# Two stores issued at once from two queues in a rotation by 180 degrees

**The chip, the cores and the metric.** The kernel runs on one core of a Trainium2 chip. The metric is the device time of one execution in microseconds (us). A program on one core has no second die to compare with, so a run counts as fast when it is within 1.5% of the fastest of its kernel; a run that stands alone has an unknown state. The span of a profile is some 1.8 us shorter than the time of the same execution.

## The reference

```python
def setup_inputs():
    batch, c, h, w = 32, 3, 256, 256
    return {"x": np.random.randn(batch, c, h, w).astype(np.float32)}

def reference(x):
    return np.rot90(x, k=2, axes=(-2, -1)).astype(np.float32)
```

There are 96 images of 65536 numbers. A rotation by 180 degrees is each image read backwards.

## The kernel before

The images go in three groups of 32. A group fills a buffer of 128 partitions: image n lies in partitions 4n to 4n+3, and a partition holds one contiguous quarter of 16384 numbers (64 KB). `inside` reverses each quarter with VectorE copies through a small buffer T, and the store writes the four quarters of each image in reverse order.

```python
    # ... cut: shapes and buffers; E = 16384 numbers per partition, J = 2048;
    # back(t, lo, hi) is columns lo to hi of t backwards, copy is a VectorE copy
    def load(t, g, lo, hi, queue=nc.sync):
        return queue.dma_start(out=t[:, lo:hi], in_=x4[g][:, lo:hi])

    def store(t, g, lo, hi):
        return nc.sync.dma_start(
            out=o4[g][:, ::-1, lo:hi], in_=t[:, lo:hi])

    def inside(t):
        for lo in range(0, E // 2, J):
            hi = E - lo - J
            copy(T[:, :], back(t, hi, hi + J))
            copy(t[:, hi:hi + J], back(t, lo, lo + J))
            copy(t[:, lo:lo + J], T[:, :])

    TAIL = 1536
    HEAD = 512
    load(A, 0, 0, HEAD, nc.scalar)
    load(A, 0, HEAD, E)
    load(Bt, 1, 0, E)
    body = load(Ct, 2, 0, E - TAIL)
    load(Ct, 2, E - TAIL, E)
    inside(A)
    LEAD = 128
    store(A, 0, 0, LEAD)
    first = store(A, 0, LEAD, E)
    tc.add_manual_dep(
        first.ins, body.ins.name,
        mybir.DependencyInfo(mybir.DependencyClass.Sync, mybir.DependencyReason.DATA),
        reason="the first store is queued while the last strip is on its way")
    for g, t in ((1, Bt), (2, Ct)):
        inside(t)
        store(t, g, 0, E)
```

Four names are used below. The head is the first 512 columns of A, loaded through ACT's queue. The body is the long part of Ct's load, the strip its last 1536 columns (rows of 6 KB). The lead is the store of A's first 128 columns (rows of 512 B), which waits in SyncE's queue behind the loads.

Of the kernel before, what the change touches and what calls it, by code (L numbers as in the profile page):

```python
# [2 lines left out]

os.environ.setdefault("NEURON_RT_ULTRASERVER_MODE", "4")

# [4 lines left out]


@with_exitstack
def kernel(
    ctx: ExitStack,
    tc: tile.TileContext,
    x: bass.AP,
    out: bass.AP,
):








    nc = tc.nc
    P = 128

    B, C, H, W = x.shape
    L = H * W
    G = 32
    E = L // 4
    J = E // 8

    x4 = x.rearrange("b c h w -> (b c) (h w)").rearrange(
        "(g n) (s e) -> g (n s) e", n=G, s=4)
    o4 = out.rearrange("b c h w -> (b c) (h w)").rearrange(
        "(g n) (s e) -> g n s e", n=G, s=4)  # L40

    pool = ctx.enter_context(tc.tile_pool(name="slots", bufs=1))
    A = pool.tile([P, E], x.dtype, tag="A")
    Bt = pool.tile([P, E], x.dtype, tag="B")
    Ct = pool.tile([P, E], x.dtype, tag="C")
    T = pool.tile([P, J], x.dtype, tag="T")

    def back(t, lo, hi):
        return t[:, hi - 1:(lo - 1 if lo else None):-1]

    def copy(dst, src):
        tc.keep_in_program_order(nc.vector.tensor_copy(out=dst, in_=src))  # L52

    def load(t, g, lo, hi, queue=nc.sync):
        return queue.dma_start(out=t[:, lo:hi], in_=x4[g][:, lo:hi])  # L55

    def store(t, g, lo, hi):
        return nc.sync.dma_start(
            out=o4[g][:, ::-1, lo:hi], in_=t[:, lo:hi])

    def inside(t):
        for lo in range(0, E // 2, J):
# [12 lines that stand above are left out]
    inside(A)  # L75
    LEAD = 128
    store(A, 0, 0, LEAD)
    first = store(A, 0, LEAD, E)
    tc.add_manual_dep(
        first.ins, body.ins.name,  # L80
        mybir.DependencyInfo(mybir.DependencyClass.Sync, mybir.DependencyReason.DATA),
        reason="the first store is queued while the last strip is on its way")
    for g, t in ((1, Bt), (2, Ct)):
        inside(t)
        store(t, g, 0, E)


# [1 line left out]
_INS = ['x']  # L89
_OUTS = [((32, 3, 256, 256), 'float32')]  # L90


# [23 lines left out]
```

## Time and profile before

| | before |
|---|---|
| time, median of 3 runs (lowest to highest) | 122.11 us (121.89 to 122.15) |
| span | 120.2 us |
| packet time of q1 (SyncE) and q10 (ACT), share of 16 DMA engines | 97.0% + 0.6% |
| VectorE busy | 44.2 us, 37% |

The prediction shows the lines of this profile that carry the argument.

### The profile page before, as it was taken

The numbers are of one execution on the slowest core, as the hardware profiler recorded it, in microseconds if no ns is written. First come the engines' busy times: TensorE is split into PE (matmuls) and PEld (weight loads), VectorE is DVE, ScalarE is ACT, GpSimd is POOL, SyncE is SP. The second block draws the span as 40 slices with busy tenths as digits, with TensorE's granted clock in tenths as the row PEclk, the third lists the DMA queues.
The fourth block names the chain that finished last, engine by engine and source line by source line (L and its number), as shares of the span: only waits on it lengthen the run. The fifth ranks groups of instructions, "written<-read, shape, count | busy, mean of one in ns | idle before, by whom it ended". The sixth has DMA issues, their size and how long they took to land.

```text
span 120.2 us, 97 instructions
## 1 busy us (share of the span) xinstructions
DVE 44.2 (37%) x36; POOL 0.2 (0%) x4
## 2 busy tenths in 40 slices
DVE  0000000499995099999059999500000000000000
POOL 0000000000000000000000000000000000000000
DMA  9888988899889879979499777988898889888990
GB/s 338 349 349 349 698 349 349 360 654 393 349 349 633 382 316 553 395 316 633 178 452 693 346 346 346 693 349 349 349 698 349 349 349 698 349 349 349 654 393 0
DMA packets 1296, 50.33 MB, mean 419 GB/s; under 512 B 144, under 2 KB 272, under 8 KB 528
## 3 DMA queue, kind: packets, MB, share of 16 engines
q1 hardware_dynamic: 1152, 50.07, 97.0%
q10 hardware_dynamic: 144, 0.26, 0.6%
HBM read 25.17 MB, written 25.17 MB: 419 GB/s over the span
## 4 chain that ended last, share of the span: by engine, by line
DMA 34%; DVE 25%; another core or an unknown queue 4%; issue 1%; SPq 0%; DVEq 0%
DMA Bt<-in_x_dram 34%; DVE T L52 8%; DVE Bt L52 8%; DVE Ct L52 8%; SPq L55 0%; DVEq L52 0%
## 5 line engine op out<-in xcount | busy, mean ns | idle before, releaser
L52 DVE COPY T<-A 128x2048 f32<-128x2048 f32 x4 | 4.9, 1226 | 22.7 <-DMA A<-in_x_dram 22.6
L52 DVE COPY T<-Ct 128x2048 f32<-128x2048 f32 x4 | 4.9, 1227 | 4.5 <-DMA Ct<-in_x_dram 4.4
L52 DVE COPY T<-Bt 128x2048 f32<-128x2048 f32 x4 | 4.9, 1226 | 4.4 <-DMA Bt<-in_x_dram 4.3
L52 DVE COPY Bt<-Bt 128x2048 f32<-128x2048 f32 x4 | 4.9, 1227 | 0.1
L52 DVE COPY A<-A 128x2048 f32<-128x2048 f32 x4 | 4.9, 1227 | 0.1
L52 DVE COPY A<-T 128x2048 f32<-128x2048 f32 x4 | 4.9, 1227 | 0.1
L52 DVE COPY Bt<-T 128x2048 f32<-128x2048 f32 x4 | 4.9, 1227 | 0.1
L52 DVE COPY Ct<-T 128x2048 f32<-128x2048 f32 x4 | 4.9, 1227 | 0.1
L52 DVE COPY Ct<-Ct 128x2048 f32<-128x2048 f32 x4 | 4.9, 1227 | 0.1
L100 POOL MEMSET const-bfloat16-1.0<- 128x1 bf16 x1 | 0.1, 101 | 0.0
L100 POOL MEMSET const-uint8-127<- 128x1 uint8 x1 | 0.1, 101 | 0.0
L100 POOL MEMSET const-float32-0.0<- 128x1 f32 x1 | 0.1, 98 | 0.2 <-issue 0.2
L100 POOL MEMSET const-float32-1.0<- 128x1 f32 x1 | 0.1, 98 | 0.0
## 6 DMA issues: line engine op xcount, KB each, us to landing
out_dram<-A SPq DMA_DIRECT2D x1, 8128.0 KB, 21.1
A<-in_x_dram SPq DMA_DIRECT2D x1, 7936.0 KB, 21.9
Ct<-in_x_dram SPq DMA_DIRECT2D x1, 7424.0 KB, 57.9
Ct<-in_x_dram SPq DMA_DIRECT2D x1, 768.0 KB, 59.3
A<-in_x_dram ACTq DMA_DIRECT2D x1, 256.0 KB, 22.0
out_dram<-A SPq DMA_DIRECT2D x1, 64.0 KB, 35.2
Bt<-in_x_dram SPq DMA_DIRECT2D x1, 40.8
out_dram<-Bt SPq DMA_DIRECT2D x1, 39.8
```

The lines of the kernel that those rows point to most:

```text
L52: tc.keep_in_program_order(nc.vector.tensor_copy(out=dst, in_=src))
L100: nc = _bacc.Bacc("TRN2", target_bir_lowering=False, num_devices=1)
```

## The change

The intent is to run the first two stores side by side: A's on SyncE's queue as before, Bt's on ACT's. Both are held until the body has landed, so that neither gets among the loads. Ct's store stays on SyncE's queue.

```diff
--- before.py
+++ after.py
@@ -54,9 +54,9 @@
     def load(t, g, lo, hi, queue=nc.sync):
         return queue.dma_start(out=t[:, lo:hi], in_=x4[g][:, lo:hi])
 
-    def store(t, g, lo, hi):
-        return nc.sync.dma_start(
-            out=o4[g][:, ::-1, lo:hi], in_=t[:, lo:hi])
+    def store(t, g, lo, hi, queue=nc.sync):
+        return tc.keep_in_program_order(queue.dma_start(
+            out=o4[g][:, ::-1, lo:hi], in_=t[:, lo:hi]))
 
     def inside(t):
         for lo in range(0, E // 2, J):
@@ -75,14 +75,18 @@
     inside(A)
     LEAD = 128
     store(A, 0, 0, LEAD)
-    first = store(A, 0, LEAD, E)
-    tc.add_manual_dep(
-        first.ins, body.ins.name,
-        mybir.DependencyInfo(mybir.DependencyClass.Sync, mybir.DependencyReason.DATA),
-        reason="the first store is queued while the last strip is on its way")
-    for g, t in ((1, Bt), (2, Ct)):
-        inside(t)
-        store(t, g, 0, E)
+    inside(Bt)
+
+    def held(dma):
+        tc.add_manual_dep(
+            dma.ins, body.ins.name,
+            mybir.DependencyInfo(mybir.DependencyClass.Sync, mybir.DependencyReason.DATA),
+            reason="the stores are queued while the last strip is on its way")
+
+    held(store(A, 0, LEAD, E))
+    held(store(Bt, 1, 0, E, nc.scalar))
+    inside(Ct)
+    store(Ct, 2, 0, E)
 
 
 # ---- launch: one core; inputs and outputs as the reference has them ----
```

## The prediction

> **What bounds the kernel now.** The kernel moves three groups of images, 8.39 MB each, from HBM into the buffers A, Bt and Ct, reverses each row of 16384 numbers inside the buffer with VectorE copies, and stores the buffers with the rows of each image in reverse order. I read the page's busy row and its DMA part first, to see which resource has no room.
>
> ```profile
> DVE 44.2 (37%) x36; POOL 0.2 (0%) x4
> ...
> DMA packets 1296, 50.33 MB, mean 419 GB/s; under 512 B 144, under 2 KB 272, under 8 KB 528
> ...
> q1 hardware_dynamic: 1152, 50.07, 97.0%
> q10 hardware_dynamic: 144, 0.26, 0.6%
> ```
>
> VectorE works for 37% of the span, while the packets of the two DMA queues take 97.0 + 0.6 = 97.6% of the time of all 16 DMA engines (q1 belongs to SyncE, q10 to ACT). The packet counts say how a transfer is cut: nine DMAs of 144 packets each, which is one packet for each of the 128 partitions and 16 small ones (the 144 under 512 B) that end it on the 16 engines. So a large DMA is 8 whole rows of about 64 KB on each engine. In the trace's packet records a row of 65536 B takes 2.418 us, in either direction: 27.1 GB/s for an engine, 434 GB/s for 16.
>
> Next the order of the transfers, from the page's list of DMA issues, put together with the start of each issue in the timeline.
>
> ```profile
> out_dram<-A SPq DMA_DIRECT2D x1, 8128.0 KB, 21.1
> A<-in_x_dram SPq DMA_DIRECT2D x1, 7936.0 KB, 21.9
> Ct<-in_x_dram SPq DMA_DIRECT2D x1, 7424.0 KB, 57.9
> Ct<-in_x_dram SPq DMA_DIRECT2D x1, 768.0 KB, 59.3
> A<-in_x_dram ACTq DMA_DIRECT2D x1, 256.0 KB, 22.0
> out_dram<-A SPq DMA_DIRECT2D x1, 64.0 KB, 35.2
> Bt<-in_x_dram SPq DMA_DIRECT2D x1, 40.8
> out_dram<-Bt SPq DMA_DIRECT2D x1, 39.8
> ```
>
> ```profile
> 59.63 0.55 SPq L58 DMA_DIRECT2D out_dram<-A  x1
> 60.27 0.55 SPq L58 DMA_DIRECT2D out_dram<-Bt  x1
> 61.55 1.23 DVE L52 COPY T<-Ct 128x2048 f32<-128x2048 f32 x1 [4.40 <-DMA Ct<-in_x_dram]
> ...
> 76.68 0.54 SPq L58 DMA_DIRECT2D out_dram<-Ct  x1
> ```
>
> Issue plus landing time gives: A loaded at 22.6, Bt at 1.18 + 40.8 = 42.0, the long part of Ct at 1.63 + 57.9 = 59.5, its last strip at 2.11 + 59.3 = 61.4; A stored at 59.63 + 21.1 = 80.7, Bt at 60.27 + 39.8 = 100.1, Ct at 76.68 + 42.7 = 119.4. The landings step by 19.4 us, and 8 rows at 2.418 us are 19.34 us: six groups pass through one first-in-first-out stream without a hole. The packet records confirm it: the first data packet starts at 1.755 us, the last completion packet at 119.05 us, and the packets in between fill the 16 engines but for 0.06 us on the average engine. Thus 120.2 us = 1.76 before the first packet + 117.3 of packets + 1.13 after the last. The pure floor of bytes is 50.33 MB / 434 GB/s = 116.0 us. In the chain of waits this looks as if VectorE carried a quarter of the span; those copies lie beside transfers that fill the engines anyway.
>
> **What the Trainium skill says.** Four places bear on it. "DMA: Bandwidth & Descriptors", section "Issuing engines are not separate DMA queues", says that transfers from SyncE and ACT end up on the same 16 DMA engines and interleave, and that a second issuer only saves issue time. Its section "Where 436 GB/s comes from" puts the ceiling at 435.2 GB/s; this trace, with 434 GB/s inside a packet, sits on it. Its section "Queues, rings and completion order" says each DMA engine goes round robin between queues and switches at packet boundaries. The trace agrees and shows the grain: the 256 KB head of A, alone in ACT's queue and worth 8 x 0.084 us per engine, lands 22.0 us after its issue, with A's 7936 KB body (21.9 us), because on each engine its 2 KB rows go one at a time between the body's 62 KB rows, in bursts about 2.4 us apart (4.8, 7.2, 9.6 ... 21.7 us). Last, "Latency and other measured facts" tells of HBM copies that slow when rows of a tile lie at large power-of-two pitches; the two stores that now run together lie exactly 8.39 MB apart, but no record of this kernel shows a slowdown, and I use it only for a rival.
>
> **The change, part by part.**
>
> 1. *Bytes and rows.* Nothing removed, nothing added: nine DMAs, 50.33 MB, 36 copies of 1.227 us. Change 0 us.
>
> 2. *Bt's store goes to ACT's queue.* SyncE's second issue (0.55 us at 60.27) disappears from SyncE and about 0.5 us appears on ACT, which has been idle since 1.1 us. It was hidden: A's store had 8 x 2.40 = 19.2 us of rows in front of it. Gain 0 us.
>
> 3. *The handover from loads to stores.* The hold ends at the same event, the landing of Ct's long part. Now A's rows arrive 60.843 - 59.63 = 1.21 us after the issue starts, when the engines are just finishing the strip and the 64 KB lead; the earliest engine waits some 0.17 us, the rest less. With both issues at about 59.6, Bt's rows come at about the same 60.8. If two simultaneous issues hinder each other, this could cost an estimated 0.1 to 0.3 us; the pair of issues at 0.73 us (0.38 and 0.39 us, each as long as a lone one) speaks against it. I choose +0.1 us.
>
> 4. *The strip's landing.* This is where something moves. At 60.8 us some engines still have a strip packet in flight and its 4-byte completion unsent, and it now takes turns with 64 KB rows of Bt. Each turn costs 2.42 us. By the records, only completions or at most one strip row are unstarted at 60.8, so one or two turns: the strip lands at 61.5 + 2.4 to 4.9 = 63.9 to 66.4 rather than 61.5. Ct's twelve copies take 76.68 - 61.55 = 15.13 us, so its store is issued at 79 to 81.6 instead of 76.7.
>
> 5. *Does that delay cost?* A and Bt together keep the engines in work from 60.8 to 60.8 + 16 rows x 2.41 = 99.4, with the small remainders about 99.7. Ct's store must be issued 1.2 us before: by 98.4. The slack is 98.4 - 76.7 = 21.7 us. Even all eight strip rows of an engine, one turn each, would cost 8 x 2.42 = 19.4 us. Hidden in either case: 0 us.
>
> 6. *The end.* Ct's eight rows are last and alone, as before: 99.7 + 19.35 = 119.05, then the same 1.13 us. A and Bt share turns, so A lands near 100 rather than 80.7; nobody needs it.
>
> Sum: 122.11 + 0.1 - 0 = about 122.2; I put 122.1, since +0.1 is no larger than the spread of the three runs (121.89 to 122.15).
>
> **The rivals.**
>
> *Two queues are faster than one.* For it, only that SyncE's queue carries 97.0% of the packet time and ACT's lies idle. Against it: that time belongs to engines which both queues share, the rows leave no gap, and the end of one DMA costs one 9 ns packet. It cannot give 2%: 2.4 us is nearly all there is outside the packets (1.76 + 1.13 us), and neither piece is touched. It would make 121.9.
>
> *The strip waits so long that Ct's store comes late.* For it, the head of A, held up to 22 us by the same turns. Against it, the 21.7 us of slack. If it happened with several microseconds over, 124 to 126.
>
> *Alternating stores write slower,* through the 8.39 MB offset or through a cost at each change of queue. Against it: 16 engines already write at 16 places at once, and the alternation of the head and A's body left no measurable idle time from 5 to 21 us. A 5% loss over the 39 us in which two stores run would be 2 us: 124.
>
> *The copies of Ct are put behind the stores by the new program order.* Those stores are issued at 60, before Ct lands: nothing.
>
> **Range and chances.** Gains end at 0.2 us; plausible losses are 0.1 to 0.3 us at the handover; the rivals with 2 us or more get 3% together. So 122.1, with 121.7 to 122.5 for 8 in 10; faster by over 2% 0.5%, within 2% 96.5%, slower 3%.
>
> **What the profile afterwards would show.** Right: ACT's queue q10 with 288 packets and 8.65 MB, its share up by 128 x 2.42 / (16 x 120.2) = 16.1 points to about 16.7%, q1 down to about 81%, the sum still 97 to 98% (step 1); the issues of A and Bt both near 59.6 (step 3); the first copy of Ct at 63.9 to 66.4 and its store issued at 79 to 81.6 (step 4); A and Bt both landing some 40 us after issue (step 6); Ct's store landing at 119.4. Wrong would be: rows of stores longer than 2.42 us, holes in the DMA row near 60 or 100 us, or Ct's store issued after 98.

## More of the kernel before

The stretches view has, after the stretch and its length, the busy time of VectorE and GpSimd in it, the granted clock, the DMA share and the GB/s. A packet is counted where it starts, so a share can pass 1 when many long rows start in one stretch. This is the kernel before, from 60 us on:

```profile
60.00:80.00 20.00, 14.72 (x12) 0.00 (x0) 1.00 1.01 434
80.00:90.00 10.00, 0.00 (x0) 0.00 (x0) 1.00 1.17 505
90.00:100.00 10.00, 0.00 (x0) 0.00 (x0) 1.00 1.01 439
100.00:118.00 18.00, 0.00 (x0) 0.00 (x0) 1.00 0.94 408
```

All 16 engines are full through the whole store phase, whether VectorE works (60 to 80 us) or not.

## The result, and the profile after

| | before | after |
|---|---|---|
| median of 6 fast runs (lowest to highest) | 122.01 us (121.89 to 122.15) | 122.07 us (121.98 to 122.12) |
| ratio, 95% interval | | 1.0004 (0.9991 to 1.0017) |
| span of the profile | 120.2 us | 120.3 us |

A ratio is the mean time of one kernel's fast runs over the mean of the other's of the same rounds, so it is not quite the ratio of the medians. The change does nothing to the time that six runs can show.

The queues of the kernel after, with packets, MB and share of the 16 engines' time:

```profile
q1 hardware_dynamic: 1008, 41.68, 80.9%
q10 hardware_dynamic: 288, 8.65, 16.7%
```

Bt's store, 8.39 MB, has moved to ACT's queue, and the sum is 97.6% as before. Its list of DMA issues (KB, us from issue to landing) and its timeline at the handover from loads to stores:

```profile
out_dram<-A SPq DMA_DIRECT2D x1, 8128.0 KB, 40.5
...
out_dram<-Bt ACTq DMA_DIRECT2D x1, 40.6
```

```profile
59.78 0.55 SPq L58 DMA_DIRECT2D out_dram<-A  x1
59.81 0.61 ACTq L58 DMA_DIRECT2D out_dram<-Bt  x1
61.70 1.23 DVE L52 COPY T<-Ct 128x2048 f32<-128x2048 f32 x1 [4.33 <-DMA Ct<-in_x_dram]
...
76.83 0.54 SPq L58 DMA_DIRECT2D out_dram<-Ct  x1
```

The stores do run side by side. They are issued 0.03 us apart, and A, which before landed after 21.1 us, now takes 40.5 us, because every second row of an engine is Bt's. Both land at 100.3 to 100.4 us; before, Bt alone landed at 100.1. Ct's copies start at 61.70 and its store is issued at 76.83, 0.15 us later than before, about as much later as the whole handover. The stretches of the kernel after show engines that are as full as before:

```profile
60.00:80.00 20.00, 14.72 (x12) 0.00 (x0) 1.00 1.01 435
80.00:90.00 10.00, 0.00 (x0) 0.00 (x0) 1.00 1.07 463
90.00:100.00 10.00, 0.00 (x0) 0.00 (x0) 1.00 1.10 477
100.00:118.00 18.00, 0.00 (x0) 0.00 (x0) 1.00 0.94 408
```

The trace also holds a record of every DMA packet, with queue, size, start and duration; no view of the profile prints them, and they do not name the engine, so what follows what on an engine is read from ends and starts that meet. A large row is one record, and a DMA ends on each engine with a completion packet of 4 bytes. In these records all 16 engines do a row of A, then one of Bt, then one of A, with 2.41 us between starts, and no row is slower for it: the mean is 2405 ns for A's rows of 65024 B (before 2403) and 2424 ns for Bt's of 65536 B (before, over all three large DMAs of such rows, 2420).

So the time came out as forecast. One step did not: the strip was to wait for a row of Bt, and Ct's copies were to start at 63.9 to 66.4. They started at 61.70.

### The profile page after: what moved, and what is told of

Its sections match the earlier page's. It is cut to its first block, busy times and chain, and to the rows that moved or that the text cites. A ratio compares the mean times of both kernels' runs of the same rounds, so it can differ in the third digit from the quotient of the medians.

```text
span 120.3 us, 97 instructions
## 1 busy us (share of the span) xinstructions
DVE 44.2 (37%) x36; POOL 0.2 (0%) x4
## 3 DMA queue, kind: packets, MB, share of 16 engines
q1 hardware_dynamic: 1008, 41.68, 80.9%
q10 hardware_dynamic: 288, 8.65, 16.7%
## 4 chain that ended last, share of the span: by engine, by line
DMA 34%; DVE 25%; another core or an unknown queue 4%; issue 1%; SPq 0%; DVEq 0%
DMA Bt<-in_x_dram 34%; DVE T L52 8%; DVE Ct L52 8%; DVE Bt L52 8%; SPq L55 0%; DVEq L52 0%
## 6 DMA issues: line engine op xcount, KB each, us to landing
out_dram<-A SPq DMA_DIRECT2D x1, 8128.0 KB, 40.5
```

## The experiments

**The theory:** the engines' packets bound the time, a queue is only a way to them, and whatever delays Ct's store by less than 21.7 us is hidden. **The rivals:** the copies of Ct lie on the path, as the chain of waits shows them; the order in which the queues are served matters; or stores and loads that take turns have a price of their own, which the hold keeps away. "Change" is the kernel after. Each diff is against it unless another is named. Every kernel gave correct results.

### How late Ct's store may come

Useless copies ahead of Ct's push its store back, in one run to just inside the slack, in one beyond it.

```diff
+    for _ in range(18):     # e7: 24
+        copy(T[:, :], back(Bt, 0, J))
     inside(Ct)
```

> The changed kernel with 18 more copies of 128x2048 (1.23 us each, result unused) ahead of Ct's copies: they start at 57.4 and fill VectorE until 57.4 + 18 x 1.261 = 80.1, so Ct's store is issued near 95.2 instead of 76.8. Theory (slack of 21.7 us): cost 0, 122.1 us. Rival (the copies of Ct lie on the path, as the chain of waits shows them): up to 18 us more.

> The same with 24 copies: Ct's copies start at 57.4 + 30.3 = 87.6, the store is issued near 102.8, its first row comes near 104.0, and the engines have run dry at 99.8. Theory: 4.2 us more than the changed kernel, 126.3. Rival (no edge at 98.5): 122 or over 130.

Over four fast runs each, 18 copies took 122.26 us, a ratio to the kernel before of 1.0025 (1.0008 to 1.0042), and 24 copies took 126.35 us, 1.0352 (1.0337 to 1.0367). The timeline has the store of Ct with 18 copies at

```profile
95.11 0.54 SPq L58 DMA_DIRECT2D out_dram<-Ct  x1
```

and with 24 copies at

```profile
102.76 0.54 SPq L58 DMA_DIRECT2D out_dram<-Ct  x1
```

With 24 copies the stretches view shows the hole between the end of A's and Bt's stores and the start of Ct's:

```profile
99.00:104.00 5.00, 3.66 (x3) 0.00 (x0) 1.00 0.22 92
104.00:122.00 18.00, 0.00 (x0) 0.00 (x0) 1.00 1.02 441
```

A store that is 18.3 us later than in the change costs at most some 0.2 us; one that is 25.9 us later costs 126.35 - 122.07 = 4.3 us, where 4.2 was worked out from engines that run dry at 99.8. Ct's first row comes at 103.95, as forecast (104.0). The edge lies where the sum put it, and the copies of Ct are off the path, although the chain shows them on it. The 0.2 us with 18 copies is not explained: its profiled run ends its last packet at 119.03 us, no later than before (119.06).

### What becomes of a store that is not held

```diff
-    held(store(Bt, 1, 0, E, nc.scalar))
+    store(Bt, 1, 0, E, nc.scalar)
```

> Bt's store in ACT's queue is not held: it is issued when Bt's copies end, near 57.4 us instead of 59.8. Theory (turns of whole rows, hidden by slack): its 64 KB rows come near 58.6 us, before the strip, and each of the strip's 8 rows per engine waits for one row of Bt, 8 x 2.42 = 19.4 us: the strip lands near 80 instead of 61.5, Ct's copies start near 80 and its store is issued near 95.5, still before 98.5, the last moment at which it costs nothing; the time stays within 0.3 us of the kernel before (122.0). Rival (a queue that comes later does not take turns with rows that are already in the other): the strip lands near 61.5 to 64, Ct's store is issued at 77 to 79, same time. Rival (the slack is smaller than worked out): 123 to 126 us.

The four fast runs took 122.69 us, a ratio of 1.0055 (1.0040 to 1.0070). The timeline is that of the first rival (Ct's store at 77 to 79), but none of the three had forecast a loss of 0.6 us.

```profile
57.32 0.63 ACTq L58 DMA_DIRECT2D out_dram<-Bt  x1
59.72 0.55 SPq L58 DMA_DIRECT2D out_dram<-A  x1
62.15 1.23 DVE L52 COPY T<-Ct 128x2048 f32<-128x2048 f32 x1 [4.87 <-DMA Ct<-in_x_dram]
...
77.28 0.54 SPq L58 DMA_DIRECT2D out_dram<-Ct  x1
```

Bt's store is issued at 57.32, about when the forecast had it, but the strip lands in time for copies at 62.15, not 80. In the packet records no row of Bt starts before 61.09 us: on each engine it comes after all eight strip rows and all eight lead rows, 52 KB that stood in SyncE's queue, and after their completion packets too, but for one that came behind a row of Bt (64.16). So my turns of whole rows did not happen to the strip. It was slowed in another way: its rows took 313 ns on average instead of the change's 234, and 8 x 0.079 = 0.63 us is about the loss (122.69 - 122.07 = 0.62).

### Do simultaneous issues hinder each other, or is ACT's path slow?

In the change each engine's first row of A came ahead of its first row of Bt. I asked why, with six single looks (one run each, so of unknown state), each beside one or more runs of the kernel before.

```diff
 # e2
-    held(store(A, 0, LEAD, E))
-    held(store(Bt, 1, 0, E, nc.scalar))
+    held(store(A, 0, LEAD, E, nc.scalar))
+    held(store(Bt, 1, 0, E))
 # e3
-    LEAD = 128
+    LEAD = 2048
 # e4: as e3, and as e5
 # e5: "held" takes the load to wait for; strip is the last load of Ct
+    held(store(A, 0, LEAD, E), strip)
+    held(store(Bt, 1, 0, E, nc.scalar), body)
```

> A's held store in ACT's queue, Bt's in SyncE's. In the changed kernel SyncE's row was first on all 16 engines and ACT's first rows began only at 63.43, behind it. If ACT's path is the slower one, or SyncE's queue is served first, Bt's rows (SyncE) come first near 61.0 and A's second near 63.4. If the one whose issue starts first wins, the order follows the issue starts. Time about 122.1 under every theory.

> The changed kernel with a lead of 2048 numbers (8 KB rows, 0.31 us each, 8 per engine, 2.5 us in all) in SyncE's queue, so that the engines still work on small rows from 61 to 63.5 and the first row of Bt shows when it comes. Both held stores are issued near 59.8. Three theories of why Bt's rows came after A's: (a) the two simultaneous issues are served one after the other: Bt's first row near 61.4 or later, some 0.4 to 0.6 us later than A's would be; (b) ACT's path is slower by itself: the same here; (c) Bt was there at 61.0 as well and SyncE's queue was served first: Bt's first row near 61.0 here, among the small rows. Time about 122.1.

> The same long lead, but A's store is held until the strip has landed (near 61.5), so that Bt's issue on ACT at 59.8 is alone. (a) served one after the other: Bt's first row 1.2 us after the issue starts, near 61.0; (b) ACT's path slower: 1.55 us or more after it, as with both; (c) 1.2 us after. Some strip completions then wait one turn of 2.42 us under (a) and (c): strip at 63.9. Time about 122.1.

> The changed kernel (short lead) with A's store held until the strip has landed, Bt's held as before and alone. (a) and (c): Bt's first rows near 61.0, the strip's completion delayed by one turn on the late engines, landing near 63.9, and A's store issued then; (b): Bt's rows at 61.4 or later, the strip lands near 61.5, the engines idle 0.3 to 0.7 us. Time 122.1 to 122.8.

With the queues swapped (122.16 us) SyncE's rows, now Bt's, came first again, and ACT's at 63.49; but SyncE's issue had also started 0.02 us earlier, so it tells little. With Bt's store alone (122.28, the run of before beside it 122.18), its first row came at 61.17, 1.26 us after its issue started at 59.91; A's on SyncE takes 1.20 to 1.21 us. Some engines stood idle when it came, so this is its arrival. ACT's path is slower by some 0.05 us, not by the 0.35 us that theory (b) needs. The strip was again in time: Ct's copies started at 61.79, not after 63.9.

The two runs with the long lead (123.09 and 123.16) missed their question: Bt's rows came only from 63.94 and 63.46 us on, long after any theory has them arrive. They showed two other things. One is a loss of 0.9 to 1.0 us, which is taken up below. The other is how turns begin. Not all lead rows went ahead of Bt: 5 of the 128 in the first run (66.39 to 69.12 us) and 12 in the second (65.88 to 69.21) started only after a row of Bt on their engine, one lead row between two rows of Bt, and 15 and 11 of the lead's 16 completion packets came as late. With one queue for all stores, all 128 lead rows had started by 64.47 us (the run comes below). So the turns that I had forecast do exist, but they begin only behind a limited amount of work of the other queue; what sets that amount is not shown.

The other two looks hold both stores until the strip has landed, so that the engines are empty, and split A's so that small rows come first.

```diff
-    held(store(A, 0, LEAD, E))
-    held(store(Bt, 1, 0, E, nc.scalar))
+    held(store(A, 0, LEAD, 640), strip)      # e11: 256
+    held(store(A, 0, 640, E), strip)         # e11: 256
+    held(store(Bt, 1, 0, E, nc.scalar), strip)
```

> Both stores are held until the strip has landed, so that the engines are idle when they are issued, and A's is in two parts, first 2 KB rows (8 x 0.084 = 0.67 us per engine), then the rest. The first rows of both show when each transfer comes. (a) Two simultaneous issues are served one after the other: Bt's first row 0.4 us or more after A's first. (b) They are served side by side: within 0.15 us, alternating with A's 2 KB rows. The engines idle for some 1.2 us, so the time is 123.2 to 124.

> As the run with both stores held until the strip has landed, but the first part of A's store has rows of 512 B (8 x 0.027 = 0.22 us per engine) instead of 2 KB. There Bt's first row followed the last of A's 2 KB rows at once, 0.68 us after A's first, which both theories allow. (a) Two simultaneous issues are served one after the other: Bt's first row still comes 0.5 to 0.7 us after A's first, after an idle gap of 0.3 us or more. (c) Bt's transfer is there at nearly the same time and goes behind what the engine has taken of A's: Bt's first row 0.2 to 0.3 us after A's first, with no gap. Time 123.2 to 124 under both.

The times were 123.90 and 123.98 us, the price of engines idle for 1.8 us (forecast 1.2). In the first look A's 2 KB rows began at 62.67 and Bt's first row at 63.35, straight behind the eighth. That fitted both theories, hence the second look: with 512 B rows, A's began at 62.69 and Bt's at 62.98. Bt's row came about 0.09 us after A's completion packet, a small gap that (c) did not have (in the first look it was 0.01 us), and far less than the 0.3 us of (a). Bt's issue had started at 61.58, so it was there at most 1.40 us later, against 1.26 alone. Serving the issues one after the other (0.5 to 0.7 us, with a gap) is refuted; a delay of up to 0.14 us remains possible. The small rows of A went first together, all eight of them, and that was not the alternation of single rows that I had forecast. In the change, then, A's rows are first probably because Bt's issue starts 0.03 us later and takes 0.05 us longer; no run shows this by itself.

### What a store among the loads costs

First, whether the loss with the long lead belongs to the second queue. This run is the kernel before, one queue for all stores, with that lead alone.

```diff
-    LEAD = 128
+    LEAD = 2048
```

> The kernel before, one queue for all stores, with the lead of 2048 numbers. In the two runs with this lead and in the run with Bt's store not held, the strip's 6 KB rows took 343, 353 and 313 ns on average instead of 234, and the times were 1.0, 1.0 and 0.65 us longer. Theory (a store with rows of 8 KB or more standing ready behind or beside the strip slows it, in whatever queue it stands): strip rows near 345 ns here too, 8 x 0.11 = 0.9 us, time near 123.0, although ACT stores nothing. Rival (the second queue does it): 234 ns and 122.1.

It took 123.07 us, 1.0082 (1.0067 to 1.0097), over four fast runs. Ct's copies start late, and both stores are on SyncE:

```profile
59.69 0.55 SPq L58 DMA_DIRECT2D out_dram<-A  x1
60.33 0.74 SPq L58 DMA_DIRECT2D out_dram<-Bt  x1
62.79 1.23 DVE L52 COPY T<-Ct 128x2048 f32<-128x2048 f32 x1 [5.54 <-DMA Ct<-in_x_dram]
```

Strip rows took 358 ns instead of 235: 8 x 0.123 = 0.99 us. That is as much as the medians differ (1.00), but this profile is of the slowest of the four runs (123.26): its last packet ends 1.27 us later than before, and the rest is engines that finish less evenly. ACT stores nothing here, so the cause is not a second queue; it is the larger lead that stands ready while load rows are still on their way. The slow strip rows (over 300 ns) start between 58.5 and 61.1 us, before the first lead row starts at 61.56, so no packet of the store need have begun. With 512 B rows (the kernel before) the strip rows are not slowed. Whether the size of the rows or the bytes of the lead count was not separated.

Second, a large dose: A's store on ACT without a hold, in the middle of the loads.

```diff
-    held(store(A, 0, LEAD, E))
-    held(store(Bt, 1, 0, E, nc.scalar))
+    store(A, 0, LEAD, E, nc.scalar)
+    held(store(Bt, 1, 0, E))
```

> A's store goes through ACT's queue and is not held: issued when A's and Bt's copies allow, at 37.8 us or soon after, in the middle of the loads, whose rows of 64 and 58 KB still have 22 us to go; Bt's store is in SyncE's queue, held as before. The run with Bt's store not held showed that it went behind all the small rows of strip and lead, so the turn of a whole row that I forecast did not come. Theory (an engine has already taken a limited amount of work from the queue in use; whole rows still take turns with what comes after that): A's rows begin one or two rows after their arrival at 39.1, so at 40 to 44, then alternate with the load rows; the long part of Ct lands near 78.8 instead of 59.5, the strip near 80.8, Ct's copies run from 81 to 96, its store is issued near 96.0, still before 98.5, and the time is 122.0 to 123. Rival (whatever is in the queue in use goes first altogether): A's rows begin only at 61, Ct lands at 61.5 and its store is issued at 77; the time then is 122.0 to 122.8.

It took 132.07 us, the median of four runs of which one was slow (133.68). The three fast ones, 131.58 to 132.25, are 1.081 times the kernel before (122.07); the recorded ratio, 1.0863 (1.0794 to 1.0933), fits only if the slow run is counted in. The theory missed this by 9 us. First, the issues and the stretches of this run; compare 434 GB/s between 60 and 80 us in the kernel before.

```profile
out_dram<-A ACTq DMA_DIRECT2D x1, 8128.0 KB, 50.2
...
Ct<-in_x_dram SPq DMA_DIRECT2D x1, 7424.0 KB, 86.1
```

```profile
60.00:80.00 20.00, 0.00 (x0) 0.00 (x0) 1.00 0.92 345
80.00:90.00 10.00, 0.00 (x0) 0.00 (x0) 1.00 0.86 329
```

Store rows begin at 44.6 to 45.1 us, one load row after the one in progress when they arrived (some 39.0), and then a row of A and a row of Ct take turns, as forecast. But the rows become slow: Ct's body rows take 2829 ns on average instead of 2206, A's store rows 2524 instead of 2403, strip rows 287 instead of 235. Eight of each per engine give 5.0 + 1.0 + 0.4 = 6.4 us. Holes of 2.6 us per engine between 64 and 100 us and engines that finish less evenly (0.6 us) make 9.6, and the last packet ends at 128.7 instead of 119.1. Of the holes, 2.0 us lie between 82 and 90 us: engines that are done early with A and Ct wait for Bt's store, whose hold ends only when all of Ct's body has landed (first row of Bt at 89.03). Those 2.0 us are thus a wait at the hold and only indirectly the slow rows. VectorE's copies are not the cause of the slow rows: it is idle from 60 to 80 us, and Ct's rows that start there take 2816 ns. Nor is Ct's late store the cause of the loss: it is issued at 105.37, but Bt's, issued at 87.83, keeps the engines full until 108.5.

Third, a control for "two queues take turns during the loads", in which both transfers are loads. The diff is against the kernel before.

```diff
-    load(Bt, 1, 0, E)
+    load(Bt, 1, 0, E, nc.scalar)
```

> The kernel before with Bt's load in ACT's queue, beside A's in SyncE's, so that two loads with rows of 62 and 64 KB take turns from 2 to 41 us; the stores stay in one queue. With A's store among the loads, the load rows of 58 KB took 2829 ns instead of 2206 and the time was 132. Theory (only a load and a store in turns slow each other, two queues as such cost nothing): A's and Bt's load rows stay near 2.42 to 2.45 us, both land near 41, the copies of A, Bt and Ct follow one another from 41.5, Ct's store is issued near 87, before 98.5, and the time is 122.0 to 122.3. Rival (turns of large rows from two queues are slow as soon as HBM reads are in them): load rows of 2.8 us, both landing near 47, 125 us or more.

It took 122.09 us, 0.9999 (0.9981 to 1.0016). The stage was not quite the one that I forecast: the head of A stands ahead of Bt in ACT's queue and is done only with A, so Bt's rows took turns with Ct's, from 22 to 59 us, instead of with A's. For the comparison that is better still, as they are the same rows of Ct as in the run before.

```profile
Ct<-in_x_dram SPq DMA_DIRECT2D x1, 7424.0 KB, 58.5
...
Bt<-in_x_dram ACTq DMA_DIRECT2D x1, 58.7
```

Ct's rows took 2193 ns with load rows of another queue in between, and 2829 ns with store rows in between. Two stores in turns (the change) and two loads in turns (this run) cost nothing; a load and a store in turns do. Why they do is not settled by these runs: the store's writes to HBM, its reads of the buffer and the changes of direction on an engine were not taken apart.

## Why the prediction was right, point by point

**Bytes and rows: right.** ACT's queue has 288 packets, 8.65 MB and 16.7%, SyncE's 80.9%, as worked out.

**The issue on ACT: right.** 0.61 us on an idle engine, with no effect on the time.

**The handover: right in size, though the time cannot show it.** A's first row comes 60.989 - 59.78 = 1.21 us after its issue, as before. Between 58 and 64 us the engines idle 0.03 us on average, where before the average shows none; the difference of the medians, 0.06 us, is within the interval. The look with 512 B rows bounds what two issues can do to each other by 0.14 us.

**The strip's landing: wrong.** The step that failed is that the strip's completion "now takes turns with 64 KB rows of Bt", one or two turns of 2.42 us. There was none. The head, from which I took the grain of the turns, had been queued at the same moment as A's body. Bt's store comes when an engine already has work of SyncE's queue before it, and a limited amount of that goes first: the 52 KB of strip and lead all did, even when Bt was issued 2.4 us early; of the long lead 5 or 12 rows of 128 did not, and these did take turns of 2.42 us with Bt. So the turns were not wrong in kind; they were applied to rows that went first. The forecast of 63.9 to 66.4 us for Ct's copies should have been 61.7. The time was spared either way.

**The slack: right.** The edge is where 98.4 was put: 95.11 costs at most some 0.2 us, and the 4.3 us that 102.76 costs lead back to 102.76 - 4.3 = 98.5. The neighbouring claim, that even eight turns would be free, was not tested as such: the turns did not come when Bt was not held, and that run lost 0.62 us by slower strip rows.

**The end: right.** A and Bt land at 100.3 and 100.4, Ct's rows follow alone, and the span is 120.3.

**The rivals.** A faster second queue is refuted by 1.0004 (0.9991 to 1.0017). Ct's copies were not put behind the stores: they start at 61.70, when the strip has landed. Stores that slow each other are refuted by their rows of 2405 and 2424 ns. What I had not listed is a store that slows a load. The held form of the change avoids it: A's first row starts at 60.99 us, when the last strip rows are under way, and strip rows keep their 234 ns. The forecast "within 2%" rested on the hold more than I knew; without it the same idea costs 0.6 us (Bt's store) or 10 us (A's store). As far as this cost goes, that was luck: the hold was taken over from the kernel before, and the prediction uses it only to say when the stores begin.

## What to carry to other kernels

This is one kernel, so take it as what to test first. When the packet records show DMA engines without a gap, ask of a change only whether it removes bytes, fills a hole or makes rows slower; the second queue for stores did none of these here. Work out how late each store may be issued before the engines run dry, and test that edge with useless work on both sides of it. Do not let large stores stand ready among loads that still run (0.6 to 10 us here): hold them until the loads have almost landed, and keep anything that must be queued earlier small.

## What the Trainium skill lacked or had wrong

- "DMA: Bandwidth & Descriptors", section "Queues, rings and completion order", gives round robin between queues at packet boundaries. It does not say in rows or bytes how much of the queue in use still goes ahead of a transfer that comes second: Bt's store, issued at 57.32 us, began at 61.09 or later, after 16 small rows (52 KB); with the long lead 5 or 12 of 128 lead rows came only between its rows; among rows of 58 to 64 KB, A's store began one row after the one in progress.
- The same section speaks of some 9 to 17 descriptors drained before the switch; once both queues had work, these runs switched after each row of 64 KB, every 2.41 us. The records do not show how many descriptors a row is, so they neither confirm nor refute the figure.
- No page that I found says that loads and stores in turns on an engine slow each other: load rows of 58 KB took 2829 instead of 2206 ns and the kernel 132.07 us, against 2193 ns and 122.09 us with loads in turns.
- Nothing wrong was found in the section "Issuing engines are not separate DMA queues" of the same page: two stores on two queues gave a ratio of 1.0004.
